# Attention on Trainium2: query norm factors on the scores instead of the query tiles, distances scaled by GpSimd, a fourth score buffer

## The chip, the cores and the metric

The kernel runs on one core of one Trainium2 chip. The metric is the device time of one execution in microseconds (us). Of the kernel before, three runs are shown: 1923.87, 1925.37 and 1925.83 us, median 1925.37. All arithmetic is in float32; a product of matrices is made of three TensorE passes (hi x hi, hi x lo, lo x hi), for which each operand is split into a rounded part, hi, and the rest, lo.

## What is computed

Two layers on an input of 1024 tokens x 1024 channels. Layer 0 mixes tokens by a short gated convolution, layer 1 by sliding-window attention; each is followed by a SwiGLU channel mixer. The change lies in the attention of layer 1. Cut to that:

```python
q = rmsnorm(q, q_gain)          # per head of 64 channels
k = rmsnorm(k, k_gain)
scores = einsum('bnqkgd,bnskd->bnkgqs', qb, kw) * scale
dist = qi + BLOCK - kj          # blocks of 128 queries against 256 keys
mask = (dist >= 0) & (dist < WINDOW) & (key_pos >= 0)
scores = scores - slopes * dist
scores = where(mask, scores, -inf)
logits = concatenate([scores, sink_col], axis=-1)
p = softmax(logits)[..., :-1]
out = einsum('bnkgqs,bnskd->bnqkgd', p, vw)
return out @ w_o
```

There are 16 query heads, 4 key/value heads, a window of 128 keys, and for each head a slope and a sink. The norm factor of a query is 1 / sqrt(mean(q^2) + eps), one number for each token and head.

## The kernel before, in words

Everything is laid out with channels on the 128 partitions and tokens along the free axis. The 16 query heads make eight *query tiles* of two heads each (i = 0 to 7). A *unit* (i, b) is the work of one query tile with one block b of 128 queries: 64 units, in order of i and then b. In a unit the two heads are handled for 64 queries at a time (two halves, called `sub`), so a score tile has 64 queries of each head on its 128 partitions and up to 192 keys along the free axis. A tile has two blocks of 4 x 128 tokens, `h` = 0 and 1.

A *step* of the attention stage (`step`, L2388) issues, for the current unit n and those before it, a fixed series of pieces, written as a string of letters in ORDER (L60). S: score matmuls of unit n into the single PSUM bank P0 (`scores`, L2226). P: a piece of the query projection of later tiles, or of the output projection. T: the probabilities of unit n-2 are transposed on TensorE (`turn`, L2271). M: on VectorE, `maxima` (L2238) reads the scores, adds the scaled distances and takes the maximum, with the sink as a bound, and writes the result into a score buffer. E: on ScalarE, `exponents` (L2262). D: divisions of finished output blocks by the softmax sums (`divide_steps`), whose factors are also widened by GpSimd (`spread`, L1800) and turned by TensorE (`turn_blocks`, L1805). k and K: whatever was planned for this step (`plan`). H, L: the hi and lo parts of the turned probabilities, on ScalarE (L2284) and VectorE (L2290). V, O: probabilities times values on TensorE, kept by ScalarE and VectorE (L2321, L2322). The order on every engine is the order in which the code is written: the stage stands in a manual schedule, and each engine works its queue in order.

`keep_q` (L2126) prepares a query tile. ScalarE squares the raw tile, TensorE sums the squares per head (`head_stats`, L1675), VectorE and ScalarE form the factor of each token and head by a logarithm, an exponential and one Newton step (`head_mean`, `head_log`, `head_guess`, `head_newton`), and VectorE multiplies it by the reciprocal of the head's slope (L1706). The factor has tokens on the partitions, while the tile has channels there. So GpSimd widens it to 128 x 512 (L1803; for tile 0 ScalarE does), TensorE turns that in four transposes of 128 x 128 (L1808), and VectorE multiplies half the raw tile by the turned factors (`scale_rows`, L1810, multiplication at L1813). This happens twice per tile, once for each `h`. Then ScalarE makes the hi parts (L2165) and GpSimd the lo parts (L2170), four of each per tile.

`maxima` then computes, in one VectorE instruction for each `sub` (L2249), (scores + dist) x (-slope), with `dist` a constant of the distances, negative, and -1e30 outside the window. The result is written into one of three score buffers in turn (`s_bufs`), of which one is a tile of its own and two are halves of G2.

Also on GpSimd's queue in this stage: the lo parts of weights (`split_granule`, L1941, whose hi cast is L1940 on VectorE; later L147), of the keys (`part`, L1878) and of the attention output (L2432), the widening of the softmax factors, and small sums for the sinks. SP issues the loads. X0 to X7 are the residual tiles of 128 x 1024; in the attention stage they lie idle from the time that the operands of layer 1 are formed until `add_x` (L287) adds the output projection to them.

Of the kernel before, what the change touches and what calls it, by code (L numbers as in the profile page):

```python
# [41 lines left out]
C_INVS = C_KG + 1  # L42
C_NEGS = C_INVS + NH
# [16 lines left out]
ORDER = "SPTMEDkPHLVOPK"  # L60
# [28 lines left out]
def trunk_kernel(ctx: ExitStack, tc: tile.TileContext, xT, small, w_in, w_out, w_q, w_v, w_o, w_gu, w_dn, out):  # L89
# [748 lines left out]
    xres = [tc.dram_tile((P, T), F32, name=f"xres{m}") for m in range(NK)]  # L838
    first_sums = [tc.dram_tile((4, GROUP, P, 5 * P), F32, name=f"s1_{l}") for l in range(2)]
# [820 lines left out]
    def attention_layer():  # L1660
# [39 lines left out]
        def head_guess(y, inv):  # L1700

            act.activation(y, y, AF.Exp, scale=-0.5)
            t = slot("hr_t", (P, NB, 2), bufs=2)
            dve.tensor_tensor(t, y, y, ALU.mult)
            if inv is not None:
                dve.tensor_tensor(y, y, inv.unsqueeze(1).to_broadcast([P, NB, 2]), ALU.mult)  # L1706
            return t
# [4 lines left out]

        it = {}
# [96 lines left out]
        def scale_rows(raw, wide, q, pb):  # L1810
            turn_blocks(pb, wide)
            c = slice(q * 512, q * 512 + 512)
            dve.tensor_tensor(raw[:, c], raw[:, c], pb, ALU.mult)  # L1813

        s_bufs = []

        def score_buffers():
            g2 = slot("G2")
            s_bufs.append(slot("s0", (P, 2, 2 * P)))
            s_bufs.extend(g2[:, h * 512 : h * 512 + 512].rearrange("p (e c) -> p e c", e=2) for h in (0, 1))  # L1820
            for s in s_bufs:
                pool.memset(s[:, 0, KEYS:], 0.0)
                pool.memset(s[:, 1, 0:SUB], 0.0)

        def keys_and_values():
# [18 lines left out]
            at(t - 20.0, constants)  # L1844
            for q in (0, 1):
# [13 lines left out]
            def token_rows():  # L1859
# [3 lines left out]
                dve.tensor_scalar(it["eps"], m, EPS, None, ALU.mult)  # L1863
                rsqrt(it["r"], m, (P, NB))
# [135 lines left out]
        def first_pairs():  # L2000
# [20 lines left out]
            def guess(g):  # L2021
                s["t", g] = head_guess(s["y", g], None)
# [39 lines left out]
            for j in range(n_first):  # L2062
                begins[j] = line.end
                u, k = seq[j]
                for p in range(NK // 2):
# [9 lines left out]
                    if (j, p) == (12, 2):  # L2075
                        for d, f in ((0.1, first.mean), (0.5, first.guess), (0.9, first.newton), (1.2, first.wide0), (2.9, first.wide1)):
# [40 lines left out]
            at(t - 0.5, first.hi0)  # L2117
            at(t - 0.5, first.hi1)
            at(t - 0.3, first.lo0)
            at(t - 0.3, first.lo1)  # L2120
            for pair in (0, 1):
                at(t + 0.1, keep_v, 1, pair)
            for d, f in ((0, first.rows1), (1, first.hi2), (1.5, first.hi3), (2, first.lo2), (3, first.lo3)):
                agenda.setdefault(d, []).append(f)

        def keep_q(i, raw_of, side=None, later=0, steps=False):  # L2126
# [16 lines left out]
            def mean():  # L2143
                t["m"] = head_mean(t["st"])
                t["y"] = head_log(t["m"])

            def guess():
                t["t"] = head_guess(t["y"], cst[:, C_INVS + 2 * i : C_INVS + 2 * i + 2])

            def newton():  # L2150
                head_newton(t["y"], t["t"], t["m"])
# [20 lines left out]
            rows_of = lambda h: scale_rows(t["raw"], t["side"][h], h, bank(pos["free"]))  # L2172
            wide_of = lambda h: spread(pool, t["side"][h], t["y"][:, 4 * h : 4 * h + 4, :])

            if steps:
                shared = lambda h: spread(act, t["side"][h], t["y"][:, 4 * h : 4 * h + 4, :])
# [7 lines left out]
                    wide0=lambda: shared(0),  # L2184
                    wide1=lambda: shared(1),
                    rows0=lambda: rows_of(0),
                    rows1=lambda: rows_of(1),
# [9 lines left out]
            first, rows = 1, (4.5, 5.5)  # L2197
            for d, fs in (
                (first, [lambda: squares(0)]),
                (first + 0.5, [lambda: squares(1)]),  # L2200
                (1.5 + first, [stats_of, mean]),
# [471 lines left out]
```

## Time and profile before

| what | value |
|---|---|
| device time, median of three runs | 1925.37 us |
| span of the profiled execution, first to last instruction | 1921.5 us |
| attention units, first scores to the end of the softmax work | about 1027 to 1230 us of the span |
| granted TensorE clock, whole span | 1.000 |
| moved by DMA | 374.13 MB, mean 195 GB/s |

For the profiled execution the profile gives its span; the 3.9 us between it and the median is time before the first and after the last instruction, and the difference between one execution and another. In the profile PE is TensorE's matmuls, PEld its weight loads, DVE VectorE, ACT ScalarE, POOL GpSimd, SP SyncE. `out<-in` names tiles with buffer numbers left out (G stands for all of G0 to G11, P for the PSUM banks). A row of a group gives count, busy microseconds, mean nanoseconds of one, and the idle time before with what ended it. Records of matmuls overlap, so their durations are longer than the time by which each moves the queue.

### The profile page before, as it was taken

To read this page: it belongs to the slowest core of one execution; us is meant where nothing else is said; L and a number is where in the kernel's file an instruction comes from. 1 tells how busy PE (TensorE), PEld (TensorE's weight loads), DVE (VectorE), ACT (ScalarE), POOL (GpSimd) and SP (SyncE) were. 2 spreads that over 40 slices of the span, in tenths; PEclk is the share of its full clock that TensorE was granted. 3 is DMA by queue.
4 is the path that set the end of the run, shared out by engine and by line. 5 is a ranking of instruction groups with operands and counts; after the bars stand their busy time and mean duration, and the time that the engine had idled before them with its cause. 6 is when DMAs were issued, how large, how long until landed. Compare 5 with 4: busy or idle time off the path is not lost.

```text
span 1921.5 us, 25423 instructions
## 1 busy us (share of the span) xinstructions
PE 1910.4 (99%) x9045; PEld 1595.6 (83%) x9045; DVE 1323.1 (69%) x2293; ACT 891.6 (46%) x1753; POOL 305.9 (16%) x391
## 2 busy tenths in 40 slices
PE   9999999999999999999999999999999999999999
PEld 7888888888888888888887888888888888888887
DVE  8998877975655666555767888788756665665543
ACT  5543464633333334444557787556333333344441
POOL 0011231011111100000015556310111111100000
PEclk9999999999999999999999999999999999999999
DMA  8896695387888647986374661232675575477562
GB/s 317 258 251 149 133 249 160 110 274 209 228 250 234 152 141 281 325 249 211 102 257 158 210 214 50 94 137 89 216 204 144 196 200 158 130 251 269 198 228 100
DMA packets 154910, 374.13 MB, mean 195 GB/s; under 512 B 15392, under 2 KB 26784, under 8 KB 154784
## 3 DMA queue, kind: packets, MB, share of 16 engines
q1 hardware_dynamic: 119392, 263.16, 40.1%
q0 software_dynamic: 35248, 109.33, 23.4%
q8 instruction: 71, 1.16, 0.2%
q14 instruction: 55, 0.45, 0.1%
q10 hardware_dynamic: 144, 0.03, 0.0%
HBM read 300.89 MB, written 149.42 MB: 234 GB/s over the span
## 4 chain that ended last, share of the span: by engine, by line
PE 96%; DVE 2%; ACT 1%; issue 1%; POOL 0%; DMA 0%; SPq 0%; POOLq 0%; ACTq 0%; DVEq 0%
PE acc L1004 16%; PE acc L1007 16%; PE acc L1005 16%; PE P L1004 10%; PE P L1005 10%; PE P L1007 10%; PE acc L172 3%; PE acc L1997 2%; PE P L1997 2%; PE acc L176 1%; PE P L2277 1%; PE P L1678 1%; PE P L1808 1%; PE acc L1137 1%; PE acc L1139 1%; PE acc L1138 1%
## 5 line engine op out<-in xcount | busy, mean ns | idle before, releaser
L1004 PE MATMUL acc<-XS,G 128*128 128x512 f32 x926 | 360.4, 389 | 0.0
L1005 PE MATMUL acc<-XS,G 128*128 128x512 f32 x926 | 360.2, 389 | 0.0
L1007 PE MATMUL acc<-XS,G 128*128 128x512 f32 x926 | 360.2, 389 | 0.0
L1004 PE MATMUL P<-A,G 128*128 128x512 f32 x550 | 214.1, 389 | 0.0
L1007 PE MATMUL P<-A,G 128*128 128x512 f32 x550 | 214.0, 389 | 0.0
L1005 PE MATMUL P<-A,G 128*128 128x512 f32 x550 | 214.0, 389 | 0.0
L1007 PEld LDWEIGHTS acc<-XS,G 128*128 128x128 f32 x926 | 173.8, 188 | 36.2
L1005 PEld LDWEIGHTS acc<-XS,G 128*128 128x128 f32 x926 | 173.8, 188 | 36.1
L1004 PEld LDWEIGHTS acc<-XS,G 128*128 128x128 f32 x926 | 173.8, 188 | 36.0
L1004 PE MATMUL acc<-A,G 128*128 128x512 f32 x442 | 172.1, 389 | 0.0
L1007 PE MATMUL acc<-A,G 128*128 128x512 f32 x442 | 172.0, 389 | 0.0
L1005 PE MATMUL acc<-A,G 128*128 128x512 f32 x442 | 171.9, 389 | 0.0
L938 DVE TENSOR_TENSOR G<-WL,G 128x512 fp32r<-128x512 f32 x168 | 115.2, 685 | 73.2 <-ACT G L937 73.2
L938 DVE TENSOR_TENSOR G<-WR,G 128x512 fp32r<-128x512 f32 (+1 forms) x216 | 144.4, 668 | 30.6 <-ACT G L937 30.6
L937 ACT CAST G<-WR 128x512 fp32r<-128x512 f32 (+1 forms) x216 | 130.5, 605 | 62.3 <-PE acc L1007 31.4
L937 ACT CAST G<-WH 128x512 fp32r<-128x512 f32 (+1 forms) x174 | 104.6, 601 | 88.5 <-PE acc L1007 38.2
L938 DVE TENSOR_TENSOR G<-WH,G 128x512 fp32r<-128x512 f32 (+1 forms) x174 | 115.6, 665 | 23.3 <-ACT G L937 23.2
L1339 ACT ACTIVATE G<-G 128x512 f32<-128x512 f32 x88 | 55.8, 634 | 158.5 <-DVE G L1436 152.7
L1007 PEld LDWEIGHTS P<-A,G 128*128 128x128 f32 x550 | 103.2, 188 | 21.5
L1004 PEld LDWEIGHTS P<-A,G 128*128 128x128 f32 x550 | 103.2, 188 | 21.4
L1005 PEld LDWEIGHTS P<-A,G 128*128 128x128 f32 x550 | 103.2, 188 | 21.4
L901 POOL DMA_DIRECT2D s<-s x68 | 60.0, 892 | 365.3 <-DMA s<-s 179.5
(414 smaller groups left out, 3794.2 us busy)
## 6 DMA issues: line engine op xcount, KB each, us to landing
G<-h SPq DMA_DIRECT2D x70, 512.0 KB, 4.5
s<-in_w_dn SPq DMA_DIRECT2D x32, 704.0 KB, 8.4
h<-X POOLq DMA_DIRECT2D x44, 512.0 KB, 4.8
s<-s POOLq DMA_DIRECT2D x32, 704.0 KB, 7.1
WR<-s SPq DMA_DIRECT2D x79, 256.0 KB, 3.9
WR<-in_w_gu SPq DMA_DIRECT2D x36, 512.0 KB, 5.1
WH<-in_w_gu SPq DMA_DIRECT2D x36, 512.0 KB, 4.2
XS<-q_ops SPq DMA_DIRECT2D x36, 512.0 KB, 5.1
```

The costliest lines, as they stand in the source:

```text
L172: pe.matmul(ps.half(h), wh, xs[:, j, c], start=first and j == 0, stop=False)
L176: pe.matmul(ps.half(h), wl, xs[:, 0, c], start=False, stop=last)
L901: nc.gpsimd.dma_start(dst[to], dst[of], accum_op=ALU.add)
L937: lambda: act.copy(out_hi, raw),
L938: lambda: lo_eng.tensor_tensor(out_lo, raw, plain(out_hi), ALU.subtract),
L1004: pe.matmul(ps, w[:, 0, c], x[:, 0, :], start=start and e == 0, stop=False, skip_group_check=True)
L1005: pe.matmul(ps, w[:, 0, c], x[:, 1, :], start=False, stop=False, skip_group_check=True)
L1007: pe.matmul(ps, w[:, 1, c], x[:, 0, :], start=False, stop=last, skip_group_check=True)
L1137: pe.matmul(ps, hi[:, kc], xs[:, 0, c], start=k == 0, stop=False, skip_group_check=True)
L1138: pe.matmul(ps, hi[:, kc], xs[:, 1, c], start=False, stop=False, skip_group_check=True)
L1339: state["silu"] = act.activation(x, x, AF.Silu)
L1997: pe.matmul(ps, g[:, w, c], x[:, b, :], start=begin and i == 0, stop=end and i == 2, skip_group_check=True)
```

## The change

The query tiles are no longer multiplied by their factors; the scores are. With y the factor of a token and head and m = mean(q^2) + eps (so that m times y is 1/y), the kernel now computes (scores + dist x slope / y) x (-y) where it had (scores / slope x y + dist) x (-slope).

- The widening, the turning and the multiplication of query tiles are gone (`scale_rows`, `rows_of`, `wide_of`), for all eight tiles and both halves. The hi and lo parts are made of the raw tile. In the plan of `keep_q` they stand after the raw tile instead of after the turned factors; `hold` puts those of tile 1 back by 2.5 steps.
- The factor must have the score tile's layout: 64 queries of each head on the partitions. `query_mean` forms the mean in that layout by four instructions on 64 partitions instead of one on 128, from a copy of eps in the same layout (`eps_q`, four small copies, once). `query_newton` yields -y (`minus`) and slope / y (`away`).
- A new piece A, in ORDER after k, issues `distances` for the next unit: GpSimd writes `dist` times `away`, one instruction for each `sub`, into the score buffer. `maxima` reads the distances from there and writes its result to the same place; its factor is `minus`.
- A fourth score buffer lies in the room of X7. X7 is copied to DRAM (`x_aside`) while the values are projected, and read back when output tile 2 is begun. When the query projection has ended, the fourth buffer moves to the room of XS0.
- The reciprocal slopes leave the constants.

The core of the diff:

```diff
-ORDER = "SPTMEDkPHLVOPK"
+ORDER = "SPTMEDkAPHLVOPK"
...
-        def head_guess(y, inv):
+        def head_guess(y):
...
-            if inv is not None:
-                dve.tensor_tensor(y, y, inv.unsqueeze(1).to_broadcast([P, NB, 2]), ALU.mult)
...
+        def query_mean(st):
+            m = slot("hr_m", (P, NB, 2), bufs=2)
+            src = st[:, 0 : 2 * NB].rearrange("p (b h) -> p b h", h=2)
+            for e in range(2):
+                to = slice(e * SUB, (e + 1) * SUB)
+                for sub in range(2):
+                    of = slice(sub * SUB, (sub + 1) * SUB)
+                    dve.scalar_tensor_tensor(m[to, :, sub], src[of, :, e], 1.0 / HD, it["eps_q"][to, :, sub], ALU.mult, ALU.add)
+            return m
+
+        def query_newton(i, y, t, m):
+            dve.scalar_tensor_tensor(t, t, 0.5, m, ALU.mult, ALU.mult)
+            dve.scalar_tensor_tensor(y, t, 1.5, y, ALU.subtract, ALU.mult)
+            minus[i] = y
+            away[i] = slot("away", (P, NB, 2), bufs=3)
+            dve.scalar_tensor_tensor(away[i], m, cst[:, C_NEGS + i : C_NEGS + i + 1], y, ALU.mult, ALU.mult)
...
-        def scale_rows(raw, wide, q, pb):
-            turn_blocks(pb, wide)
-            c = slice(q * 512, q * 512 + 512)
-            dve.tensor_tensor(raw[:, c], raw[:, c], pb, ALU.mult)
...
+        def another_buffer():
+            s_bufs[3] = slot("XS0", (P, 2, D))[:, 0, lo_half].rearrange("p (e c) -> p e c", e=2)
+            clear_margins(s_bufs[3])
+
+        def last_x_back():
+            X[NK - 1] = slot(f"X{NK - 1}")
+            nc.sync.dma_start(X[NK - 1], x_aside)
...
+            s_bufs.append(slot(f"X{NK - 1}")[:, lo_half].rearrange("p (e c) -> p e c", e=2))
...
+            at(t + 9.0, lambda: nc.sync.dma_start(x_aside, X[NK - 1]))
...
-                    if p == 1 and j == 13:
-                        line.work(2, first.rows0)
...
-            first, rows = 1, (4.5, 5.5)
...
-                (rows[0] - 1.5, [lambda: wide_of(0)]),
-                (rows[0] - 0.5, [lambda: wide_of(1)]),
-                (rows[0], [lambda: rows_of(0)]),
-                (rows[0] + 0.5, [lambda: part_hi(0, 0)]),
-                (rows[1], [lambda: rows_of(1), lambda: part_lo(0, 0)]),
...
+            for d, f in ((1, lambda: squares(0)), (1.5, lambda: squares(1)), (2.5, stats_of), (2.5, mean), (3, guess), (3, newton)):
+                plan(d + later, f)
+            for n, (h, e) in enumerate(((0, 0), (0, 1), (1, 0), (1, 1))):
+                d = later + hold + 2 + n + 0.5 * (n > 0)
+                plan(d, lambda h=h, e=e: part_hi(h, e))
+                plan(d + (0.5 if n else 1), lambda h=h, e=e: part_lo(h, e))
...
+        def distances(i, b):
+            s = s_bufs[(i * NB + b) % 4]
+            for sub in (0, 1):
+                _, n = sub_keys(b, sub)
+                end = (3 + sub) * SUB
+                pool.tensor_scalar(s[:, sub, end - n : end], dist[:, KEYS - n :], away[i][:, b, sub : sub + 1], None, ALU.mult)
...
         def maxima(i, b):
             u = S[i, b]
-            s = s_bufs[(i * NB + b) % 3]
+            s = s_bufs[(i * NB + b) % 4]
...
-                    dist[:, KEYS - n :],
-                    cst[:, C_NEGS + i : C_NEGS + i + 1],
+                    live,
+                    minus[i][:, b, sub : sub + 1],
...
+                "A": lambda: at(-1, distances),
...
-            keep_q(1, lambda: rooms["odd"], later=4)
+            keep_q(1, lambda: rooms["odd"], later=4, hold=2.5)
...
+            another_buffer()
...
+                    if m == 2 and k == 0:
+                        last_x_back()
```

Line numbers in the text and in the profile of before are those of the kernel before. In the rows of the new order the same code has other numbers: the distances are L2251, the transposes of probabilities L2292 (before L2277), the projection L2029 (L1997), the lo parts of weights L1973 (L1941), of query tiles L2200 (L2170) and of keys L1910 (L1878).

More of the change, by code (lines that the diff above doesn't have):

```diff
@@ L1863, in token_rows @@
                 dve.tensor_scalar(it["eps"], m, EPS, None, ALU.mult)
+                it["eps_q"] = slot("eps_q", (P, NB, 2))
+                for e in range(2):
+                    for sub in range(2):
+                        of = it["eps"][sub * SUB : (sub + 1) * SUB, :]
+                        dve.tensor_copy(it["eps_q"][e * SUB : (e + 1) * SUB, :, sub], of)
                 rsqrt(it["r"], m, (P, NB))
@@ L2116, in first_pairs, with keep_q @@
             t = line.end
[L2117 to L2120, printed above, removed]
+            at(t - 1.6, first.hi0)
+            at(t - 0.9, first.lo0)
+            at(t - 0.8, first.hi1)
+            at(t - 0.1, first.lo1)
             for pair in (0, 1):
                 at(t + 0.1, keep_v, 1, pair)
[L2123 removed]
+            for d, f in ((0.5, first.hi2), (1, first.hi3), (1.5, first.lo2), (3, first.lo3)):
                 agenda.setdefault(d, []).append(f)
[L2126 removed]
+        def keep_q(i, raw_of, side=None, later=0, hold=0, steps=False):
             t = {}
```

44 lines of the change are left out of this document (13 added, 31 removed).

## Prediction

> **What bounds the kernel now.** I read the page first, then the waits of TensorE, then busy time by stretches of the attention stage, then the chain inside that stage. From the page, the busy time of TensorE and the make-up of the chain that ended last:
>
> ```profile
> PE 1910.4 (99%) x9045; PEld 1595.6 (83%) x9045; DVE 1323.1 (69%) x2293; ACT 891.6 (46%) x1753; POOL 305.9 (16%) x391
> PE 96%; DVE 2%; ACT 1%; issue 1%; POOL 0%; DMA 0%; SPq 0%; POOLq 0%; ACTq 0%; DVEq 0%
> ```
>
> TensorE sets the end nearly everywhere; a microsecond taken from its queue is worth a microsecond unless a wait takes it back. Its waits (total, times, longest) that lie in the changed stage:
>
> ```profile
> PE P L2234 <- DVE mx L2249: 2.4, 4, 1.0
> PE acc L1997 <- POOL WL L1941: 1.7, 2, 1.4
> PE P L2234 <- POOL G L2170: 0.5, 1, 0.5
> ```
>
> The scores (L2234) wait because their single PSUM bank P0 is still being read by the maxima on VectorE (L2249); the projection waits for weights split by GpSimd. By stretches (length; busy PE, PEld, DVE, ACT, POOL), from the first score to the end of the softmax work:
>
> ```profile
> 1027.00:1060.00 33.00, 29.19 (x189) 24.60 (x188) 25.78 (x75) 27.70 (x75) 22.03 (x16) 1.00 0.50 175
> 1060.00:1155.00 95.00, 93.61 (x651) 83.75 (x651) 84.11 (x251) 75.57 (x236) 54.15 (x58) 1.00 0.64 211
> 1155.00:1179.00 24.00, 24.00 (x168) 21.59 (x167) 17.84 (x57) 19.79 (x60) 16.36 (x18) 1.00 0.17 56
> 1179.00:1230.00 51.00, 50.61 (x325) 44.09 (x324) 40.94 (x116) 36.80 (x117) 22.18 (x29) 1.00 0.10 32
> ```
>
> The first 33 us hold 3.8 us of TensorE idling; the next 95 only 1.4, with VectorE 89% busy and GpSimd 57%. So three engines run close together there, and GpSimd is the one with room. The maxima alone, in two of these stretches, give the length of a step: four VectorE records belong to one unit.
>
> ```profile
> 1060.00:1155.00 95.00, 27.33 (x127) 1.00 0.64 211
> 1155.00:1179.00 24.00, 5.46 (x26) 1.00 0.17 56
> ```
>
> 127 / 4 is 32 units in 95 us, 2.97 us a step; then 3.7 us.
>
> **What leaves TensorE.** Turning the widened factors (L1808) of a query tile is two blocks of four transposes. One row of its records, and the same block on the chain:
>
> ```profile
> L1808 PE MATMUL P<-cst,G x72: 270/272/328, 997.7 to 1166.8; 128*128 128x128 f32 x72
> ...
> 1088.00 0.44 PE P L2277 x4
> 1088.44 0.44 PE P L1808 x4
> 1088.87 0.23 PE acc L1997
> ```
>
> A record lasts 272 ns, but records overlap, and four move the chain by 0.44 us: 0.11 us each. Eight tiles lose 64 transposes: 64 x 0.11 = 7.0 us, all of it in TensorE's queue. That is the first term, **-7.0 us**.
>
> **What VectorE and ScalarE lose and get.** Rows of the scaling by the turned factors (L1813), the reciprocal slope (L1706) and one mean (L1685):
>
> ```profile
> L1813 DVE TENSOR_TENSOR G<-G,P x8: 681/684/690, 1022.0 to 1167.1; 128x512 f32<-128x512 f32 x8
> L1706 DVE TENSOR_TENSOR hr_y<-hr_y,cst x8: 174/175/177, 1018.5 to 1178.0; 128x16 f32<-128x16 f32 x8
> L1685 DVE SCALAR_TENSOR_TENSOR hr_m<-P,eps_r x10: 168/174/175, 993.8 to 1175.6; 128x16 f32<-128x16 f32 x10
> ```
>
> Away go 16 scalings (two a tile, 0.68 us: 10.9) and eight of L1706 (1.4). Added are three more means a tile, one factor `away` a tile, and four tiny copies of eps once: 36 x 0.17 = 6.1. VectorE is 6.2 us lighter. The maxima keep form and count; one input is only read from another tile. ScalarE loses two copies of tile 0. The lighter VectorE should give back about half of the 1.4 us idled in the 95-us stretch: **-0.7 us**. The hi and lo parts of a query tile no longer wait for turned factors, so they are only earlier; `hold` puts tile 1's back where they stood.
>
> **What GpSimd gets.** Two distances a unit, 128 in all, 128x192 with one tensor input. The trace has no such instruction; the nearest rows, by form:
>
> ```profile
> L1941 POOL TENSOR_TENSOR WL<-WR,WL 128x512 fp32r<-128x512 f32 x22 | 28.6, 1302 | 40.1 <-ACT WL L1940 11.0 <-DVE WL L1940 8.7 <-PE P L2277 8.1
> L2170 POOL TENSOR_TENSOR G<-G,G 64x512 fp32r<-64x512 f32 x15 | 19.4, 1290 | 2.9 <-ACT G L2165 2.0
> L147 POOL TENSOR_TENSOR WL<-WR,WH 128x256 fp32r<-128x256 f32 x14 | 10.2, 737 | 18.7 <-ACT WH L144 18.5
> L1803 POOL COPY G<-hr_y 128x512 f32<-128x512 f32 x12 | 7.2, 611 | 12.0 <-PE P L1808 6.1 <-DVE hr_y L1711 5.8
> L1822 POOL MEMSET G<- 128x64 f32 x2 | 0.3, 151 | 0.4 <-PE P L1997 0.4
> ```
>
> From below, between the memset of 64 columns (151 ns) and the one-input copy of 512 (611 ns): 0.28 us at 192. From above, the two-input line through 256 columns (737) and 512 (1302): 0.60 us. I take 0.35, near the copy, which also reads one tensor, with something for the pointer operand. A pair is then 0.70 us (0.57 to 1.19). In the 95-us stretch GpSimd loses eight copies (two for each of four tiles, 4.9 us) and gets 32 x 0.70 = 22.4: 72 of 95 us, 75% (at the upper price 92%). It does not fill up; the question is when, in its queue, a pair stands. A pair for the next unit is issued one step ahead, behind whatever GpSimd was given before.
>
> That is a **new wait**: the maxima on VectorE now need GpSimd. Behind them in VectorE's queue stand the lo parts of the turned probabilities (L2290), keep_o and the weight casts; TensorE's next scores wait for the bank.
>
> On GpSimd where the first units begin (WL: projection weights; G: query lo parts; A: key lo part; s: a score buffer), before:
>
> ```order
> L1941 TENSOR_TENSOR WL_7846<-WR_7842,WL_7846 128x512
> L2170 TENSOR_TENSOR G_1200_8440<-G_1176_8270,G_1200_8440 64x8x64
> L1878 TENSOR_TENSOR A_1178_8273<-G_1161_8073,A_1177_8272 64x1024
> L1941 TENSOR_TENSOR WL_7847<-WR_7842,WL_7847 128x512
> L1941 TENSOR_TENSOR WL_7846<-WR_7842,WL_7846 128x512
> ```
>
> and now:
>
> ```order
> L1973 TENSOR_TENSOR WL_7847<-WR_7843,WL_7847 128x512
> L2251 TENSOR_SCALAR s_1189_8375<-cst_61,away_8387 128x64
> L2251 TENSOR_SCALAR s_1189_8375<-cst_61,away_8387 128x128
> L2200 TENSOR_TENSOR G_1201_8436<-G_1177_8277,G_1201_8436 64x8x64
> L1910 TENSOR_TENSOR A_1179_8280<-G_1162_8080,A_1178_8279 64x1024
> L2251 TENSOR_SCALAR G_1188_8374<-cst_61,away_8387 128x192 x2
> L1973 TENSOR_TENSOR WL_7848<-WR_7843,WL_7848 128x512
> ```
>
> Two pairs now stand ahead of the second split of WL. In the trace that run of GpSimd is unbroken, and TensorE waits for its last piece:
>
> ```profile
> 1029.00 1.29 POOL L1941 TENSOR_TENSOR WL<-WR,WL 128x512 fp32r<-128x512 f32 x1 [1.56 <-DVE WL L1940]
> 1030.36 1.36 POOL L2170 TENSOR_TENSOR G<-G,G 64x512 fp32r<-64x512 f32 x1
> 1031.80 2.39 POOL L1878 TENSOR_TENSOR A<-G,A 64x1024 fp32r<-64x1024 f32 x1
> 1034.27 1.60 POOL L1941 TENSOR_TENSOR WL<-WR,WL 128x512 fp32r<-128x512 f32 x1
> ...
> 1035.93 0.50 PE L1997 MATMUL acc<-XS,WL 128*128 128x512 f32 x1 [1.43 <-POOL WL L1941]
> ```
>
> The run grows by a short pair (64 and 128 columns, about 0.5) and a full one (0.7): **+1.2 us**. Tile 0's two blocks, 0.88 us, lie ahead of it and are in the first term.
>
> In the steady part, TensorE's order loses only the query block. Around a score step (P_12xx are PSUM tiles), before:
>
> ```order
> L1997 MATMUL acc_8414<-XS_1101_7500,WL_7847 128x512 x2
> L2277 MATMUL P_1261_8892<-cst_61,G_1187_8365 128x128 x4
> L1808 MATMUL P_1262_8904<-cst_61,G_1244_8764 128x128 x4
> L1997 MATMUL acc_8414<-XS_1101_7500,WL_7847 128x512
> L1997 MATMUL acc_8414<-XS_1106_7534,WL_7847 128x512
> ```
>
> and now:
>
> ```order
> L2029 MATMUL acc_8420<-XS_1101_7501,WL_7848 128x512 x2
> L2292 MATMUL P_1263_8915<-cst_61,G_1188_8374 128x128 x4
> L2029 MATMUL acc_8420<-XS_1101_7501,WL_7848 128x512
> L2029 MATMUL acc_8420<-XS_1106_7535,WL_7848 128x512
> ```
>
> The four L1808 rows are gone and nothing else moved. On GpSimd, in contrast, a stretch of 1.3-us pieces now stands between two pairs. From the tenth unit on, the new order has 16 places where at least 2.58 us of other work (by the rows above) stands between one pair and the next: 2.59 + 0.70 - 2.97 = 0.32 us late each, 5.1 us in all. VectorE (89%, later 74% busy) and the room ahead of the next scores take up more than half: **+2.0 us**.
>
> A second cost of a busier GpSimd shows in one place: the weight cast on VectorE (L1940, minimum, median, maximum ns), then GpSimd, VectorE and TensorE at that moment:
>
> ```profile
> L1940 DVE CAST WL<-WR x20: 411/427/1504, 1028.3 to 1157.2; 128x512 fp32r<-128x512 f32 x20
> ...
> 1150.09 1.49 POOL L2170 TENSOR_TENSOR G<-WH,G 64x512 fp32r<-64x512 f32 x1
> ...
> 1150.36 1.50 DVE L1940 CAST WL<-WR 128x512 fp32r<-128x512 f32 x1
> ...
> 1152.63 0.36 PE L2234 MATMUL P<-A,G 128*128 128x192 f32 x1 [0.58 <-DVE mx L2249]
> ```
>
> The cast took 1.09 us too long while GpSimd worked, and TensorE lost 0.58 us. But the median is near the minimum, so most casts met nothing, at 57% busy; at 75% I expect one or two more such meetings, which VectorE's 6.2 us cover. The Trainium skill (SBUF — State Buffer, "Who interferes with whom") says that copies and casts on VectorE can take the port pair shared with GpSimd, and that whoever issues first blocks the other fully. The trace agrees in this event; taken strictly for every cast, the sum would be that of the second rival below.
>
> Taken at nothing: the copy of X7 aside and back (512 KB each). Its place in SP's queue is behind the loads of the first row, after X7's last write in the second:
>
> ```profile
> 973.20 2.04 SPq L1934 DMA_DIRECT2D G<-in_w_q  x2
> ...
> L1537 DVE TENSOR_TENSOR X<-X,acc x2: 680/684/689, 943.3 to 955.6; 128x512 f32<-128x512 f32 x2
> ```
>
> It waits for nothing, and the way back ends five output tiles before X7 is added to. If it were late, the last output tile would wait some microseconds. Four memsets of 0.15 us more on GpSimd; those in XS0 wait for the last projection, which TensorE reaches anyway.
>
> **Sum.** -7.0 - 0.7 + 1.2 + 2.0 = -4.5 us. The profiled span of 1921.5 us lies 3.9 us under the median of 1925.4; I leave that difference as it is: 1925.4 - 4.5 = **1920.9**. About 0.2%, 3.9 us, is what a measurement of this kernel can tell from no change.
>
> **Rivals.** Full gain: GpSimd is never late (0.28 us each, slack enough everywhere). For it: its 25% of room. Against: the unbroken run at 1029. -7.0 - 1.4 = -8.4: 1917.0. Chance 0.13.
>
> Casts blocked: each of the 20 meets a GpSimd instruction and waits half of 1.30 us, 13.0 us in all, of which the event above has 1.1 already; half of the 11.9 reaches TensorE, as 0.58 of 1.09 did: +6.0 in place of the +2.0. -7.0 - 0.7 + 1.2 + 6.0 = -0.5: 1924.9, no change. For it: the event; against: the median. Chance 0.18; with other mixtures of small waits, no change has 0.30.
>
> GpSimd late: the distances cost 0.60 us, as two-input work does. The 16 places are late by 2.59 + 1.19 - 2.97 = 0.81 us, 13.0 us, and VectorE, bound to the scores' one bank, hands it all on: -7.0 + 1.2 + 13.0 = +7.2: 1932.6. It beats the saving from 5.8 / 16 = 0.36 us a place, or 0.37 us a distance with nothing absorbed. For it: 89% on VectorE leaves little to absorb; against: the copy's 611 ns. Chance 0.15, and 0.02 for a transfer or memset that holds GpSimd's queue.
>
> **Numbers.** The forecast has 0.40, the full gain 0.13: faster 0.53. Same 0.30, slower 0.17. The range runs from just under the full gain, 1916.5, to 1929.5, which takes in the blocked casts and half of the late case.
>
> **What would show it.** Right: 80 rows of L1808's transposes instead of 144; the distances at 0.3 to 0.4 us; GpSimd near 75% in the dense stretch; the split of WL still awaited near 1036; waits of VectorE's maxima on GpSimd of a few us in total. Wrong: distances at 0.5 us or more, casts with a median far over 0.43, or TensorE's waits for the maxima growing beyond 7 us in total.

## The result, and the profile after

The changed kernel takes 1950.34 us (median of four runs, 1948.5 to 1953.42), the kernel before beside it 1925.6 us (four runs, 1923.87 to 1926.02): a ratio of 1.0134, interval 1.012 to 1.0149. It is slower by 24.7 us, where 4.5 us of gain were forecast, and lies outside the range. The profiled execution has a span of 1946.7 us.

First the page's busy times, then the waits of the stage from 1020 to 1290 us (total, times, longest):

```profile
PE 1915.7 (98%) x8981; PEld 1592.6 (82%) x8981; DVE 1325.6 (68%) x2305; ACT 893.1 (46%) x1751; POOL 391.3 (20%) x509
```

```profile
PE P L2242 <- DVE mx L2264: 19.8, 22, 2.2
...
DVE G L2264 <- POOL G L2251: 15.9, 23, 3.1
...
DVE X L2264 <- POOL X L2251: 6.4, 10, 1.7
...
DVE s L2264 <- POOL s L2251: 4.4, 10, 2.0
```

The 64 transposes are gone (8981 matmuls against 9045). But the scores now wait 19.8 us for the maxima, against 2.4 before, and the maxima wait for GpSimd's distances, which didn't exist before: 26.7 us in these three rows (a fourth, for the distances in XS, has 3.0). The distances and the weight casts, by source line (minimum, median, maximum ns), and two groups (busy us, mean ns):

```profile
L2251 POOL TENSOR_SCALAR G<-cst,away x64: 753/763/1265, 1033.9 to 1245.2; 128x192 f32<-128x192 f32 x64
```

```profile
L1972 DVE CAST WL<-WR x20: 411/520/1262, 1027.0 to 1176.0; 128x512 fp32r<-128x512 f32 x20
```

```profile
L2251 POOL TENSOR_SCALAR G<-cst,away 128x192 f32<-128x192 f32 x64 | 49.7, 788 | 0.5
...
L2251 POOL TENSOR_SCALAR s<-cst,away 128x64 f32<-128x64 f32 x8 | 3.5, 440 | 0.1
```

A distance costs 0.76 us at the median and 0.79 on average, where the forecast had 0.35 and an upper bound of 0.60. The stretches of before, now (length; PE, PEld, DVE, ACT, POOL; granted clock):

```profile
1027.00:1060.00 33.00, 24.87 (x136) 19.76 (x135) 20.12 (x64) 21.24 (x57) 29.93 (x29) 0.90 0.37 129
1060.00:1155.00 95.00, 87.00 (x564) 73.35 (x562) 76.65 (x231) 70.92 (x215) 84.24 (x100) 0.98 0.63 208
1155.00:1179.00 24.00, 19.98 (x127) 16.79 (x127) 17.24 (x51) 15.99 (x49) 21.60 (x24) 0.96 0.29 89
```

GpSimd has 84.2 of 95 us, not the forecast's 72. How full that is shows in its timeline (start, duration):

```profile
1052.77 1.30 POOL L1973 TENSOR_TENSOR WL<-WR,WL 128x512 fp32r<-128x512 f32 x1 [1.18 <-PE P L2292]
1054.15 1.29 POOL L2200 TENSOR_TENSOR G<-WH,G 64x512 fp32r<-64x512 f32 x1
1055.53 1.50 POOL L2251 TENSOR_SCALAR X<-cst,away 128x192 f32<-128x192 f32 x2
1057.12 1.26 POOL L2200 TENSOR_TENSOR G<-WH,G 64x512 fp32r<-64x512 f32 x1
```

Between two instructions there can be a gap of 0.08 to 0.09 us (1052.77 + 1.30 = 1054.07, next at 1054.15), while the records of the two scalings of a unit follow each other without one (0.76 us each, 1.50 together). In the dense stretch such gaps sum to 2.3 us. For another 8.3 us GpSimd waits for the other engines, most of all for VectorE's weight casts:

```profile
POOL WL L1973 <- DVE WL L1972: 2.9, 3, 1.9
```

So GpSimd is nearly full, and VectorE and GpSimd wait for each other. VectorE's side of the place above:

```profile
1056.33 0.48 DVE L2264 CUSTOM_DVE_ANT_0 X<-P,X,cst 128x192 f32<-128x192 f32 x1 [1.72 <-POOL X L2251]
```

To see where the time goes, take the first score of a tile: eight units lie between two such rows. First scores of tile 1 and tile 5, before and after:

```profile
1052.57 0.30 PE L2234 MATMUL P<-A,G 128*128 128x64 f32 x1 [0.55 <-POOL G L2170]
...
1148.89 0.24 PE L2234 MATMUL P<-A,G 128*128 128x64 f32 x1
```

```profile
1058.43 0.30 PE L2242 MATMUL P<-A,G 128*128 128x64 f32 x1 [2.04 <-POOL G L2200]
...
1167.36 0.30 PE L2242 MATMUL P<-A,G 128*128 128x64 f32 x1 [1.74 <-DVE mx L2264]
```

Tile 0 ends 5.9 us later than before. Tiles 1 to 4, called the dense part below, take 108.9 us instead of 96.3: 12.6 more. The rest is lost in the last three tiles.

### The profile page after: what moved, and what is told of

Same layout as the page of the kernel before. It is cut to its first block, busy times and chain, and to the rows that moved or that the text cites. A ratio compares the mean times of both kernels' runs of the same rounds, so it can differ in the third digit from the quotient of the medians.

```text
span 1946.7 us, 25466 instructions
## 1 busy us (share of the span) xinstructions
PE 1915.7 (98%) x8981; PEld 1592.6 (82%) x8981; DVE 1325.6 (68%) x2305; ACT 893.1 (46%) x1751; POOL 391.3 (20%) x509
## 3 DMA queue, kind: packets, MB, share of 16 engines
q8 instruction: 70, 1.15, 0.2%
```

## The experiments

Three theories. *Late*: the distances stand in GpSimd's queue, and the maxima wait for them. *Load*: GpSimd's new work costs even where nobody waits for it, because its other work comes late and VectorE's operations are held up beside it. *Rest*: what the change does besides the distances (moved parts, four means, buffers) loses the time. Sixteen kernels were run; each diff is against the changed kernel.

**Does the loss belong to the distances?** e1 leaves them out; e2 computes them for nobody; e10 is e2 without them.

```diff
-ORDER = "SPTMEDkAPHLVOPK"
+ORDER = "SPTMEDkPHLVOPK"
...
-                    live,
+                    dist[:, KEYS - n :],
```

> Leaves out the scaling of the distances: GpSimd computes none, and the maxima read the unscaled distances for every query head, as a constant. All else of the change stays (64 transposes fewer, the moved splits, the regrouped means, the residual tile set aside). The late theory (the maxima wait for GpSimd's distances, 0.76 us each) and the load theory (GpSimd's 95 us of new work makes its other work late) both expect what is left of the forecast without its GpSimd terms: 1925.6 - 7.0 - 0.7 = about 1918 us, 1915 to 1922. The theory that the rest of the change loses the time (the moved splits and means, the buffer in the residual tile's room) expects that the loss stays: over 1938 us.

Measured: 1926.52 us, ratio to before 1.001 (1.0 to 1.0019). The loss is gone, so it isn't the rest of the change. But the 7.7 us that both surviving theories expected as a gain are missing too.

```diff
+            s = s_bufs[3]
...
+            s = s_bufs[(i * NB + b) % 3]
...
+                    dist[:, KEYS - n :],
```

> GpSimd computes all 128 distances as in the changed kernel and at the same places, but writes them to the fourth buffer, where nobody reads them; the maxima read the unscaled distances (left out: the factor in the scores) and go round three buffers. The late theory: nobody waits for the distances, so the 29.7 us of VectorE's waits for L2251 go, and the time falls to 1918 to 1925 us. The load theory: GpSimd is as full as before, its lo parts and split weights come as late as in the changed kernel, VectorE's casts stand as long beside it: 1938 us or more. If both hold in part, the time between 1918 and 1950 gives the shares.

Measured: 1944.39 us, 1.0104 (1.0088 to 1.0121). e10 has the last two lines of that diff and e1's ORDER:

> As e1 (no distances are computed; the maxima read the unscaled ones), but the maxima go round three score buffers, as in e2: the only thing that e2 has beside it is GpSimd's unread distances. If e2's 18 us over e1 are GpSimd's load, this stays with e1 at 1924 to 1929 us. If the missing fourth buffer makes them, this comes out near e2, at 1940 us or more.

Measured: 1927.08 us, 1.001 (1.0 to 1.0019): the buffer's number is worth nothing here. So 1944.39 - 1927.08 = 17.3 us of the loss are GpSimd's load, with nobody reading what it makes, and some 6 us (1950.34 - 1944.39) come with the waiting. Load carries most. In e2 the casts on VectorE took longer, and TensorE waited in tile 0 for a split weight instead of a maximum:

```profile
L1972 DVE CAST WL<-WR x20: 412/880/1495, 1026.9 to 1168.4; 128x512 fp32r<-128x512 f32 x20
```

```profile
1037.07 0.80 PE L2029 MATMUL acc<-XS,WL 128*128 128x512 f32 x1 [4.00 <-POOL WL L1973]
```

**How does an unread load cost 17 us?** Two variants of e2: the sink products moved to VectorE, and clears in place of the products.

```diff
-                pool.tensor_tensor(t, t, tiles.unsqueeze(1)...)
+                dve.tensor_tensor(t, t, tiles.unsqueeze(1)...)
...
-                pool.tensor_tensor(sums[p, h], sums[p, h], t, ALU.add)
+                dve.tensor_tensor(sums[p, h], sums[p, h], t, ALU.add)
```

> As e2 (GpSimd computes the distances, nobody reads them; 1944.4 us, of which e10 without them explains 1927.1), with the two small products of each sink (128x16, 16 in all) moved from GpSimd to VectorE. If the unread load costs its 17 us through the small sink products that stand late in GpSimd's queue and hold up ScalarE (12.4 us of ScalarE's waits for them in e2, 3.2 in e1), it falls to 1934 us or below. If it costs through VectorE's own operations being stretched beside GpSimd, or through late lo parts, it stays at 1941 to 1947 us.

Measured: 1944.49 us, 1.0096 (1.0081 to 1.0111). So the late sink sums, 12.4 us of ScalarE's waits in e2, don't explain the 17 us.

```diff
+            s = s_bufs[3].rearrange("p e c -> p (e c)")
+            for sub in (0, 1):
+                pool.memset(s, 0.0)
```

> As e2, but the two unread products of a unit are two clears of the unread buffer (128x512 each), which read nothing; from the rows of the clears (154 ns for 64 columns) and the copy (614 ns for 512) an estimate of 0.6 to 0.7 us each, so nearly the same occupancy of GpSimd's queue. If the occupancy of the queue is what costs (lo parts and sinks late): near e2, 1939 to 1945 us. If what costs is that GpSimd's two-way traffic stretches VectorE's operations on tiles beside it: VectorE's weight casts fall from a mean of 804 ns back to 550 or less and the time to 1928 to 1935 us.

Measured: 1936.22 us, 1.0054 (1.0038 to 1.007), between the two answers, in runs from 1932.23 to 1940.05; the mean cast took 601 ns, also between them. The clears were shorter than estimated:

```profile
L2249 POOL MEMSET X<- x90: 516/526/956, 1031.3 to 1177.2; 128x512 f32 x90
```

so the run doesn't separate occupancy from traffic. Half of the 17 us went with a third of the occupancy.

**Is it the operation's price?** e3 multiplies by a constant, e4 makes one product of two tensors.

```diff
-                pool.tensor_scalar(s[...], dist[...], away[i][:, b, sub : sub + 1], None, ALU.mult)
+                pool.tensor_scalar(s[...], dist[...], 1.0, None, ALU.mult)
```

> The distances are multiplied by the constant 1.0 in place of the factor read from the tile away (left out: the factor); same operation, same shapes, same places. If the reading of one factor per partition makes the operation dear, a 128x192 distance falls from 0.79 us to near the copy's price (614 ns for 512 columns, so some 0.25 to 0.4 us) and the time to 1918 to 1928 us. If the operation itself is dear on GpSimd, it stays at 0.70 to 0.80 us and the time at 1945 to 1953 us.

```profile
L2251 POOL TENSOR_SCALAR G<-cst x64: 680/689/1081, 1034.2 to 1243.6; 128x192 f32<-128x192 f32 x64
```

Measured: 1947.64 us, 1.0121 (1.0106 to 1.0136). With a constant a scaling takes 0.69 us in place of 0.76. The pointer accounts for a tenth of the price, and the operation is dear without it.

```diff
+            pool.tensor_tensor(both, dist.unsqueeze(1).to_broadcast([P, 2, KEYS]),
+                away[i][:, b, :].unsqueeze(2).to_broadcast([P, 2, KEYS]), ALU.mult)
```

> Same result, another operation: from the second block on, one GpSimd product of two tensors for both halves of a unit (128x384, the distances read twice, the factor spread along the columns), where two TENSOR_SCALAR stood. From the rows of TENSOR_TENSOR (735 ns for 256 columns, 1280 for 512: 2.1 ns a column, 190 ns fixed) an estimate of 1.0 us a unit, against 1.55 us. The late theory: the loss of 25 us falls with GpSimd's load, which drops by 112/2 x 0.55 = 31 of 95 us; as the queue's lateness is what is lost, more than a third of it: 1930 to 1942 us. The theory that the rest of the change loses the time: no change, 1948 to 1953 us.

```profile
L2256 POOL TENSOR_TENSOR G<-cst,away 128x384 f32<-128x384 f32 x32 | 26.5, 832 | 0.4
```

One product of 384 columns took 0.83 us, hardly more than one scaling of 192: GpSimd's new work fell from 1.53 to 0.83 us a unit. Yet the time is 1944.86 us, 1.0106 (1.0091 to 1.0121), over the expected range. VectorE, then TensorE, in e4's tile 1 show one way in which load is more than a sum:

```profile
1072.36 0.82 DVE L1704 TENSOR_TENSOR hr_t<-hr_y 128x16 f32<-128x16 f32 x1
1073.22 0.17 DVE L1724 SCALAR_TENSOR_TENSOR hr_t<-hr_t,hr_m 128x16 f32<-128x16 f32 x1
1073.43 0.69 DVE L1725 SCALAR_TENSOR_TENSOR hr_y<-hr_t,hr_y 128x16 f32<-128x16 f32 x1
1074.15 1.30 DVE L1728 SCALAR_TENSOR_TENSOR away<-hr_m,cst,hr_y 128x16 f32<-128x16 f32 x1
```

```profile
1076.52 0.50 PE L2242 MATMUL P<-A,G 128*128 128x192 f32 x1 [2.45 <-DVE mx L2269]
```

```profile
1075.00:1085.00 10.00, 8.48 (x37) 7.52 (x38) 7.03 (x21) 5.27 (x16) 5.16 (x8) 0.66 0.38 130
```

Three of these four small products of the Newton step, 0.17 us when undisturbed, took 0.7 to 1.3; the maxima queued behind them came late, TensorE paused 2.45 us, and its granted clock was 0.66 over the ten us around and after.

**Would another engine carry the distances?** In e8 VectorE scales all, in e7 ScalarE, in e9 each one of a unit, in e5 GpSimd one and ScalarE one.

The diff is e9's; the other three name other engines in its first line.

```diff
+            for sub, eng in ((0, dve), (1, act)):
...
+                if eng is act:
+                    act.activation(o, x, AF.Copy, scale=f)
+                else:
+                    eng.tensor_scalar(o, x, f, None, ALU.mult)
```

> Same result; VectorE scales all the distances, GpSimd none. From VectorE's shortest 128x512 cast (411 ns) an estimate of 0.2 us for 192 columns: 128 x 0.2 = 26 us more on VectorE, 11 us of them in the 95 us from 1060 to 1155, where e1 has it 82 us busy: 94 us, so it is full there. The load theory (GpSimd's occupancy is what costs, on whichever tile it works) expects GpSimd back at 50 us of 95 there, and 1927 to 1936 us. The theory that 128 more operations cost the same wherever they stand expects 1945 us or more.

> Same result; VectorE scales the first distance of each unit, ScalarE the second (a copy with a scale per partition), GpSimd none. From the rows 411 ns (VectorE, 512 columns) and 447 ns (ScalarE's exponential, 192 columns, of which some 350 ns are its pitch): 13 us more on VectorE and 22 us on ScalarE over the stage, in the dense stretch 88 and 87 us of 95. Load theory: 1925 to 1933 us, no more than 8 us over e1. Same cost anywhere: 1945 us or more.

> Same result; ScalarE scales all the distances (a copy with a scale per partition), GpSimd none. At 350 to 450 ns each 45 to 57 us more on ScalarE, some 21 to 24 us of them in the dense stretch, where e1 has it 78 us busy: 99 to 102 of 95 us, over full. Both theories expect it slower than e9; load theory 1932 to 1942 us.

Measured: e8 1947.22 us, 1.0114 (1.0099 to 1.0129); e9 1936.89, 1.0061 (1.0046 to 1.0076); e7 1944.98, 1.0107 (1.009 to 1.0124). All three lie above the load theory's ranges, e7 by 3 us and e9 by 4; e8 came out where the other answer had it (1945 us or more), but e9 contradicts that answer, a cost that is the same anywhere. VectorE's scaling in e8, and the dense stretch of e8 and of e7:

```profile
L2255 DVE TENSOR_SCALAR G<-cst,away x64: 225/315/1625, 1029.6 to 1245.1; 128x192 f32<-128x192 f32 x64
```

```profile
1060.00:1155.00 95.00, 87.43 (x553) 72.01 (x551) 91.36 (x284) 69.91 (x213) 43.97 (x44) 0.98 0.63 208
```

```profile
1060.00:1155.00 95.00, 86.33 (x552) 72.30 (x551) 71.07 (x224) 85.57 (x266) 42.69 (x44) 0.98 0.64 207
```

The engine that gets all of them has 84 to 91 of 95 us, whichever it is. Split between two they cost about half. None of the places tried here is free.

**Half the load.** GpSimd scales one distance of each unit, the forecast's 0.70 us a unit in truth.

```diff
-            for sub in (0, 1):
+            for sub in (0,):
...
+                far = live if sub == 0 else dist[:, KEYS - n :]
```

> Half of the changed kernel's distances: GpSimd scales the first of each unit, which its maximum reads and waits for; the second maximum of the unit reads the unscaled distances (left out: its factor). GpSimd's new work is then one operation of 0.76 us a unit, 48 us in all, which is what the forecast charged for both (0.70 a unit). If only the price of the operation was wrong in the forecast, the forecast's own terms for that load (1.2 + 2.0 us) hold over e1's 1926.5: 1929 to 1931 us. If every operation put on GpSimd here costs in proportion, half of the 24 us: 1937 to 1941 us; then the forecast was wrong on the load too, not on the price alone. Under 1933 the loss bends (it grows faster than the load), over 1941 it saturates.

> Same result as the changed kernel; GpSimd scales the first distance of each unit, ScalarE the second (442 ns each in e7). Against e15 this adds 64 x 0.44 = 28 us to ScalarE, of which e7, with twice that, lost 18 us over e1. If the two loads add up, 1926.5 + 9 (half of e7's) + what e15 has over e1; if the loop takes the later of the two, no more than 3 us over e15. Nothing here expects it under the kernel before's 1925.6.

Measured: e15 1935.57 us, 1.0051 (1.0035 to 1.0068); e5 1939.84, 1.0079 (1.0064 to 1.0094), so ScalarE's half adds 4.3 to e15, between the two answers of its expectation. Proportion (12 of 24 us) would give 1938, the forecast's terms 1930; e15 lies between, and by the mark of its expectation (under 1933) the total doesn't bend. Where the loss lies is read from the first scores of tiles 1 and 5, for e15 and then e1:

```profile
1060.92 0.30 PE L2242 MATMUL P<-A,G 128*128 128x64 f32 x1 [0.60 <-DVE G L2013]
...
1159.12 0.30 PE L2242 MATMUL P<-A,G 128*128 128x64 f32 x1 [1.01 <-DVE mx L2265]
```

```profile
1054.86 0.30 PE L2242 MATMUL P<-A,G 128*128 128x64 f32 x1 [0.53 <-POOL G L2200]
...
1150.16 0.19 PE L2242 MATMUL P<-A,G 128*128 128x64 f32 x1
```

The dense part takes 98.2 against 95.3 us: 2.9 for half the load, 13.6 (108.9) for the whole. Here it bends. But tile 0, where GpSimd's run of weights and key parts stands, is 6.1 us late already at half the load, against 3.6 in the changed kernel (1058.43). So that is not load alone: in this execution of e15 TensorE's granted clock was 0.50 for 13.7 us of tile 0, in e1's for 6.8. The room is worked out from e1's GpSimd in the dense stretch:

```profile
1060.00:1155.00 95.00, 93.08 (x629) 81.31 (x628) 82.45 (x258) 77.70 (x239) 50.53 (x51) 1.00 0.65 213
```

50.5 us and 1.0 of short gaps are taken; the other 43.5, over 32 units, leave 1.36 us a unit. One scaling needs 0.77 + 0.09 = 0.86 and fits, two need at least 1.53 and don't. The single product of e4 (0.83 + 0.09 = 0.92) fits too, and e4 still lost, so room is not all that counts.

**Where is the saving?** e13 puts 56 of the turned blocks back into e1, e14 takes the Newton products out of it.

```diff
+            for h, d in ((0, 4.5), (1, 5.5)):
+                plan(d + later, lambda h=h: turn_blocks(bank(pos["free"]), t["raw"][:, h * 512 : h * 512 + 512]))
```

> As e1 (no distances), with 56 of the 64 turned 128x128 blocks put back on TensorE at the steps at which they stood before, turning the raw query tile; nobody reads them. The forecast's term (0.11 us of TensorE each) gives + 6.2 us over e1: 1932 to 1934 us. If TensorE, waiting for the maxima there, has idle time that takes them up, or if they shorten the pauses after which its clock falls, 1924 to 1929 us: then the 7 us were never to be had.

Measured: 1932.2 us, 1.0037 (1.0025 to 1.005), 5.7 over e1: 0.10 us a transpose. The saving is real.

```diff
-            dve.scalar_tensor_tensor(t, t, 0.5, m, ALU.mult, ALU.mult)
-            dve.scalar_tensor_tensor(y, t, 1.5, y, ALU.subtract, ALU.mult)
-            dve.scalar_tensor_tensor(away[i], m, cst[...], y, ALU.mult, ALU.mult)
+            act.activation(y, y, AF.Copy, scale=-1.0)
```

> As e1 (no distances), without the Newton step of the query norm factors (left out: four small products on VectorE per tile; the sign is set by ScalarE). In e1 these 128x16 products took up to 2.22 us in place of 0.17 beside a long GpSimd operation, the maxima behind them came late, TensorE paused 2.2 and 2.8 us, and its granted clock fell to 0.5 to 0.6 behind each pause. If those pauses are what keeps e1 8 us above the forecast's 1918, this one gains 4 us or more: 1919 to 1923 us. If the pauses are only handed on, 1925 to 1929 us.

Measured: 1921.67 us, 0.9977 (0.9967 to 0.9986), as the first answer had it: 4.9 us under e1, more than half of the 8.5 that e1 lay above the forecast's 1918. So most of what e1 lacked hung on these products. (The run also takes 32 x 0.17 = 5.4 us of undisturbed work off VectorE, so it doesn't tell their meetings from their mere load.) In e1, while the units of tile 5 run, GpSimd, then VectorE, then TensorE, then the clock:

```profile
1161.83 1.30 POOL L2200 TENSOR_TENSOR G<-G,G 64x512 fp32r<-64x512 f32 x1
1163.21 1.29 POOL L2448 TENSOR_TENSOR XS<-G,XS 128x512 fp32r<-128x512 f32 x1
```

```profile
1162.01 1.15 DVE L1724 SCALAR_TENSOR_TENSOR hr_t<-hr_t,hr_m 128x16 f32<-128x16 f32 x1
...
1163.41 1.13 DVE L1728 SCALAR_TENSOR_TENSOR away<-hr_m,cst,hr_y 128x16 f32<-128x16 f32 x1
```

```profile
1165.51 0.53 PE L2242 MATMUL P<-A,G 128*128 128x192 f32 x1 [2.78 <-DVE mx L2264]
```

```profile
1164.00:1172.00 8.00, 6.49 (x24) 5.76 (x25) 5.22 (x15) 5.07 (x16) 5.55 (x9) 0.57 0.00 0
```

Both VectorE products end 0.03 to 0.04 us after the GpSimd product beside them ends (1163.16 and 1163.13; 1164.54 and 1164.50): they stood until it was done. The pause is 2.78 us, and the clock is 0.57 for 8 us.

The clock is a part of the loss that no theory above had. In e1's profiled execution it was 0.50 in these stretches:

```profile
1038.70:1042.00 3.30, 3.30 (x14) 2.81 (x13) 3.00 (x4) 2.98 (x9) 2.58 (x2) 0.50 0.13 50
1045.50:1048.90 3.40, 3.40 (x14) 2.91 (x13) 2.38 (x7) 2.25 (x4) 0.00 (x0) 0.50 0.00 0
1165.00:1171.70 6.70, 6.19 (x23) 5.51 (x24) 4.09 (x13) 3.82 (x13) 4.33 (x8) 0.50 0.00 0
```

That is 13.7 us to the edges, at most 6.8 us of TensorE's time; in e14 6.8 us, in before's profiled execution none. The times go with it: of e1's ten runs the three with a mean granted clock of 0.998 or 0.999 took 1924.4 to 1924.6 us, the seven at 0.996 or 0.997 took 1926.4 to 1931.1; of the thirteen of before beside them, the eight at 1.000 took 1923.6 to 1924.3, the five at 0.997 or 0.998 took 1925.3 to 1927.2.

**Can those meetings be avoided in a whole kernel?** The Newton products on GpSimd, in e4 (e16) and in the changed kernel (e17):

```diff
+            pool.tensor_tensor(t, t, m, ALU.mult)
+            pool.tensor_scalar(t, t, 0.5, 1.5, ALU.mult, ALU.subtract)
+            pool.tensor_tensor(y, t, y, ALU.mult)
...
+            pool.tensor_tensor(m, m, y, ALU.mult)
+            pool.tensor_scalar(away[i], m, cst[...], None, ALU.mult)
```

> Same result: e4 (one GpSimd product a unit, 0.83 us) with the small 128x16 products of the Newton step on GpSimd too (six of about 0.22 us by the row of the sink sums, 1.3 us a tile). In e4 these products, on VectorE, took up to 1.30 us in place of 0.17 beside GpSimd's new products; behind them TensorE paused 2.45, 2.59 and 3.28 us in three tiles and its clock was 0.60 to 0.71 for some 10 us. If those meetings carry e4's loss in the tiles after the first (e4's first scores of tiles 1 and 5 are 107 us apart, before's 96), the time falls by 10 to 20 us, to 1925 to 1935 us. If GpSimd's load carries it, no change: 1942 to 1947 us.

> Same result: the changed kernel (two products a unit, 1.53 us) with the Newton step's small products on GpSimd, as in e16. In the dense stretch GpSimd is busy 84 of 95 us, and with about 0.09 us between one instruction and the next (100 of them) it is full; 1.3 us a tile come on top. Theory that a full GpSimd queue sets the pace of the changed kernel: no gain, 1948 to 1955 us. Theory that the meetings with VectorE's small products carry the loss there too: 1930 to 1942 us.

Measured: e16 1947.35 us, 1.0118 (1.0102 to 1.0135), a miss: TensorE's long pauses in the dense part gave way to more and shorter ones (none over 1.3 us), which sum to 11.0 us, against 9.7 in e4. ScalarE now waits longer for the sink sums (5.5 us in e4), though by e11 such waits need not cost time:

```profile
ACT mx L2355 <- POOL mx L2354: 19.8, 8, 4.3
```

e17 takes 1968.51 us, 1.0227 (1.0212 to 1.0242), above both ranges of its expectation: six small products a tile, 1.6 us, 12.9 us in all, cost 18. A full queue alone doesn't explain it, and the hundred gaps of 0.09 us from which its expectation worked out that the queue is full aren't in the changed kernel's trace. In tiles 1 to 4 GpSimd is busy for 104.2 of 119.4 us (87%), in the changed kernel for 98.3 of 108.9 (90%); the granted clock was 0.50 for 47.8 us of the attention stage, against 13.7. What lowered it is not shown. No kernel that computes the whole result came under the kernel before.

## Why the prediction was wrong, point by point

*The transposes, -7.0.* Right: 0.10 us each by e13 against 0.11.

*The lighter VectorE, -0.7.* Wrong in kind. Counting VectorE's microseconds missed that its products on tiles in SBUF wait for GpSimd's running instruction. The parts that were "only earlier" met the Newton products: e1, without any distance, gains nothing over before, and e14 gets 4.4 us of the 7.7 back (0.23% of 1925). The forecast also had no term for the granted clock, which took up to 6.8 us of e1's profiled execution and up to 3.4 of e14's; how much of the missing 3 us it makes isn't shown.

*The price, 0.35 with 0.60 as its upper bound.* This is the step that failed first. "Near the copy, which also reads one tensor" was the wrong neighbour: a scaling took 0.76 us where the copy line gave 0.28 and the two-input line 0.60. At 1.53 us, a pair is over the room of 1.36 us a unit that e1 shows; at the forecast's 0.70 it would have fitted. By "distances at 0.5 us or more" the prediction named this as a sign that it is wrong, and by "beyond 7 us in total" another: TensorE's waits for the maxima came to 19.8.

*The queue, 75% in the dense stretch, and +2.0 for its lateness.* With the true price it is 84.2 of 95 us, 89%, and most of the rest is waiting. At the load that it assumed, e15 has 70.7 us busy, close to the forecast's 72:

```profile
1060.00:1155.00 95.00, 90.90 (x613) 79.03 (x611) 80.67 (x251) 77.77 (x240) 70.66 (x80) 1.00 0.64 214
```

and the dense part is 2.9 us longer than e1's, near the steady term of +2.0; but in e15 only half of the maxima wait for GpSimd. In e4 all of them do, at 0.83 us a unit against the forecast's 0.70, and its dense part (first scores at 1061.23 and 1168.42) is 11.9 us longer than e1's: TensorE pauses for 9.7 us there instead of 1.9, and its clock is 0.50 for 10.2 us instead of none. So the price alone did not overturn the forecast. The second step that failed is that most of a late pair would be absorbed, and that one or two more meetings of VectorE and GpSimd would be covered by VectorE's 6.2 us.

*The run at 1029, +1.2.* Mis-sized, price apart: at half the load tile 0 costs 6.1 us over e1, of which the clock's 6.8 us more at 0.50 can be up to 3.4, and in the changed kernel 3.6. The forecast looked at the split of WL alone. In the changed kernel TensorE no longer waits for that one but, three times, for the maxima:

```profile
1030.47 0.53 PE L2242 MATMUL P<-A,G 128*128 128x192 f32 x1 [2.22 <-DVE mx L2264]
1035.99 0.36 PE L2242 MATMUL P<-A,G 128*128 128x192 f32 x1 [1.92 <-DVE mx L2264]
1048.18 0.36 PE L2242 MATMUL P<-A,G 128*128 128x192 f32 x1 [1.75 <-DVE mx L2264]
```

and its clock in that stretch is 0.90.

*The rivals.* "GpSimd late" named the mechanism of the smaller part, some 6 us, that comes with reading the distances: maxima waiting for them, decisive from 0.37 us a distance. Its 13.0 us were for 0.60 us and 16 places; two scalings of a unit no longer fitted into its room, and the time ran to 1950 instead of 1932.6. "Casts blocked" was right on the casts: the median went from 427 to 520 ns, and to 880 in e2. The mean of the 20 went from 548 to 621, 1.5 us in all, and what of that reached TensorE isn't shown. The Trainium skill (SBUF — State Buffer, "Who interferes with whom") says that a VectorE instruction with two inputs in SBUF contends with a GpSimd instruction that reads SBUF, and that one with at most one such input, outside the two-port modes, doesn't. The trace agrees: the Newton products of e1 stood 1.15 and 1.13 us, while the lo parts, with one input in PSUM, keep to their time beside a full GpSimd:

```profile
L2305 DVE TENSOR_TENSOR G<-P,G x64: 417/684/693, 1039.4 to 1256.7; 128x512 fp32r<-128x512 f32 x56, 128x256 fp32r<-128x256 f32 x8
```

(before: 418/685/694). The prediction weighed this rule for casts only and asked how many casts would meet something; it should have asked for every VectorE operation between two SBUF tiles that stands ahead of a maximum.

*What stays open:* why e4 and e16, whose single product of 0.92 us with its gap fits into 1.36, still lose 18 to 21 us over e1, e16 even with the Newton products away from VectorE; how e2's 17.3 us divide between late GpSimd work and held-up VectorE operations, since e12's clears were too short to tell; and how much of each loss is the lowered clock, which no run holds fixed.

## What to carry to other kernels

Price an operation from a row of the same opcode on the same engine; if there is none, measure it first. Before giving work to an engine "with room", divide that room by the steps and see whether one step's work fits. That it fits is not enough, as e4 shows: look at what the new work will delay on the engines that wait for it, at the place where the engine already runs unbroken (tile 0 here), and, when times differ by less than 1%, at the granted clock of each run. And beside a busier GpSimd, VectorE's small products between SBUF tiles cost up to GpSimd's whole instruction: look at what is queued behind them.

## What the runs showed of the hardware that was not expected

On GpSimd one product of two tensors, spread from 192 columns and two factors to 384, takes 832 ns, one scaling of 192 columns 763 ns, and 689 with a constant in place of the pointer. On ScalarE a scaled copy of 192 columns takes 442 ns, on VectorE 225 undisturbed and up to 1625.

TensorE's granted clock, 1.00 in every stretch shown of before, fell to 0.50 for 3.4 us at a time, or two or three times as long, in the changed kernel and its variants. In e1 and e4 it mostly stood by pauses of 2.2 to 4.9 us, though in e1 it was 0.50 once already, from 1039 to 1041 us, ahead of the pause that ended at 1044.69. In e14 it came with no pause there; TensorE had just worked for 1.95 us on sixteen products of two columns, the sums of squares:

```profile
1153.24 1.95 PE L1678 MATMUL P<-cst,G 128*128 128x2 f32 x16
```

```profile
1155.00:1158.00 3.00, 3.00 (x12) 2.61 (x12) 2.39 (x11) 1.35 (x8) 2.51 (x2) 0.51 0.31 104
```

The Trainium skill (TensorE: Matmul & The Clock Gate, Part 1) has a half clock after an idle window of about 3.4 us. The half agrees; nearly all pauses here were shorter, and in e14 there was none. A series of such products also ended 1.3 us ahead of e1's fall at 1038.7, but in before's profiled execution seven of them passed without one. So what lowers the clock is not settled, and the expectation of e14, which put it down to the pauses, claimed too much.
